# Explicit order edges on VectorE and ScalarE in a hybrid SSD and pooling decoder step: row product behind state updates, last gate half behind evictions, last weights' lower halves behind the last row block

## The chip, the cores and the metric

The kernel runs on one core of a Trainium2 chip. The core has a matrix engine (TensorE, PE in the profile), three elementwise engines (VectorE or DVE, ScalarE or ACT, GpSimd or POOL) and a queue that issues most transfers (SyncE, SP). The metric is the device time of one execution in microseconds (us). Instructions on one engine run in the order in which they stand in its program; engines wait for one another through semaphores.

## The reference, cut to what matters

One inference step of a two-layer trunk, in f32, for 1024 prompt tokens and 8 samples of 8 tokens each: 1088 columns in all (model width 1024, inner width 2048). Layer 0 is a Mamba-2 SSD layer, layer 1 a multi-scale causal pooling layer; each is RMSNorm with a conditioned scale and shift, a projection, a mixer, a gate and an output product, added to the residual. The parts that the change touches:

```python
def step(h, inp):                       # SSD: state from chunk to chunk (128 tokens)
    s, d = inp
    return d[..., None, None] * h + s, h
...
y_inter = jnp.einsum('bctgn,bctgr,bcgrpn->bctgrp', C, jnp.exp(acum), h_prev)
y = (y_intra + y_inter).reshape(b, L, H, P)
...
gated = (y * jax.nn.silu(z.astype(jnp.float32))).reshape(b, L, N_GROUPS, D_INNER // N_GROUPS)
gated = gated * lax.rsqrt(jnp.mean(gated * gated, axis=-1, keepdims=True) + EPS)
gated = gated.reshape(b, L, D_INNER) * norm_g.astype(jnp.float32)
return gated.astype(h.dtype) @ w_out, new_conv, new_ssm
...
return mixed.astype(h.dtype) @ w_out, up[:, -POOL_STATE:]      # pooling layer
...
y = rmsnorm(x, final_norm_g).astype(x.dtype)
```

`gated * rsqrt(mean) * norm_g` is the row product of the title. The new states, convolution tails and pooling tails are outputs too.

## The kernel before

Activations lie with channels on the 128 partitions and the 1088 tokens along the free axis. A product in f32 precision is made of three fast matmuls: each operand is split into an upper half (ScalarE copies it to a rounded type) and a lower half (VectorE subtracts the upper half from the raw tile), and TensorE adds upper times upper, upper times lower and lower times upper.

The program has four stages: a front part (normalisation, gates and part of the input projection), the scan of the SSD layer, the rest of that layer's output product with the pooling layer's projections and mixing, and the pooling layer's output product with the final normalisation.

**The scan.** `ssd_layer` goes over 8 groups of 4 heads (groups 0 to 7). `scan_group` is a generator: it handles chunks of 128 tokens in pairs and yields between them. In `front(c)` TensorE transposes the chunk's rows (`tr`, L573 and L576), ScalarE makes the decay mask `M` (L581, L582) and copies `Bt` (L593), VectorE makes `cb` (L584), multiplies `M` by it (L587) and makes `xd` (L589). `states(c, F)` lets TensorE write the chunk states `S` (L615) and updates the running state `h`: the first one of a group is a copy of `S` (L620), later ones are `hd = h * decay` on GpSimd (L623) and `h = hd + S` on VectorE (L624). `rows(c, F)` lets TensorE form the output rows `y` from `M` and `xd` (L636) and from the state (L640), and VectorE adds them into the group's tile (L607). After the last chunk the generator has three more parts, which belong to the end of the group: the gate, squares and mean with a transfer of the reciprocal root out to memory and back, broadcast to all partitions (`rs`, L742 and L745); then **the row product**, two VectorE instructions of 128x1088 (L749), each followed by a store of its result on the SP queue (`gyd`, L752).

`ssd_layer` steps these last parts inside the next group's scan (`rest` is the previous group's generator). Beside the scan stand the fill units of `beside()`: input projections of groups 1, 2, 3, 4 and 6 (matmuls L190 to L192), then three parts of the output product. The table `FILL` says how many fill units follow each scan step. The fill's projection tiles are evicted by ScalarE (L434, L436) and convolved by VectorE and ScalarE (L366 to L372).

**The output product of the SSD layer** sums over 16 row tiles in four parts. A row tile is loaded from `gyd` (`gr`, L766) and split: `gh` on ScalarE (L771), `gl` on VectorE (L772). Part 0 is loaded by the generator `self.prep`; `op_first` uses it first, with `gh` in L796 and L797 and `gl` in L801. The projection tile just ahead of it (group 6, tile 3) is written out by hand in `proj_group`: its three column blocks are evicted together, and one more step of `self.prep` follows, which issues the split of the last row tile of part 0 (the last gate half).

**The end of the kernel.** The pooling layer's output product goes over seven block products (`ORDER`). `block_steps` makes the row blocks `b`: ScalarE the upper half (L1187), VectorE the lower half (L1188). `ow_split` makes the weights' upper halves on ScalarE (L1231) and lower halves on VectorE (L1232). Before the last block product a loop in `pool_layer` fetches and splits the weights that are still missing. `contribute` adds a finished product into the residual (L1243).

**What sets the order.** Each engine's instructions are ordered by a scheduler, which takes the program's text as priority but lets an instruction stand earlier when it counts it as ready earlier. `tc.issue_after(ins)` adds an edge: what is issued inside it may not stand ahead of `ins` on the same engine. The edge adds no wait between engines.

Of the kernel before, what the change touches and what calls it, by code (L numbers as in the profile page):

```python
# [8 lines left out]
F32 = mybir.dt.float32  # L9
# [90 lines left out]
class Build:  # L100
# [296 lines left out]
    def proj_group(self, G):  # L397

        for ii in range(4):
            w = self.stream_next()  # L400
            raw = self.proj_begin(G, ii)
            if (G["g"], ii) == (BESIDE[-1], 3):
# [28 lines left out]
    def proj_evict(self, G, ii, raw, ps, c, end=True):  # L431
        nc, (a, n) = self.nc, CH[c]
        pn = min(a + n, NP) - a
        nc.scalar.activation(raw[:, 3 + a:3 + a + pn], ps[:, :pn], AF.Identity)  # L434
        if pn < n:
            nc.scalar.activation(raw[:, 1027:1115].rearrange("p (b w) -> p b w", w=11)[:, :, 3:11],  # L436
                                 ps[:, pn:n].rearrange("p (b i) -> p b i", i=8), AF.Identity)
            if end:
                self.proj_end(G, ii, raw, True)

    def gate_chunk(self, dst, c, ps):
# [83 lines left out]
    def scan_group(self, g, T):  # L525
# [84 lines left out]
        def states(c, F):  # L610
# [5 lines left out]
            for i in range(2):  # L616
                cd, Si = F[i][5], S[:, 256 * i:256 * i + 256]
                hn = gp.tile([P, 4, 64], F32, tag="h", bufs=3, name=self.name("h"))
                if h[-1] is None:
                    nc.vector.tensor_copy(hn.rearrange("p r q -> p (r q)"), Si)  # L620
                else:
                    hd = gp.tile([P, 4, 64], F32, tag="hd", bufs=1, name=self.name("hd"))
                    nc.gpsimd.tensor_tensor(out=hd, in0=h[-1], in1=cd.unsqueeze(2).to_broadcast([P, 4, 64]), op=ALU.mult)  # L623
                    nc.vector.tensor_tensor(out=hn, in0=hd, in1=Si.rearrange("p (r q) -> p r q", r=4), op=ALU.add)  # L624
                h.append(hn)

        def rows(c, F):
# [536 lines left out]
    def block_steps(self, m, rows):  # L1164
# [13 lines left out]
        for k in range(8):  # L1178
# [8 lines left out]
            nc.scalar.activation(t[:, :HALF], src, AF.Copy)  # L1187
            nc.vector.tensor_tensor(out=t[:, HALF:], in0=src, in1=t[:, :HALF].bitcast(F32), op=ALU.subtract)  # L1188
            out.append(t)
# [346 lines left out]
    def ssd_layer(self):  # L1536
# [118 lines left out]
    def pool_layer(self):  # L1655
# [239 lines left out]
```

## Time and profile before

| What | us |
|---|---|
| Median of 3 runs | 1607.51 (1605.86 to 1612.53) |
| The profiled execution's own time | 1606.84 |
| Its span, first to last instruction | 1605.1 |
| TensorE busy | 1579.7 |
| VectorE busy | 1292.1 |
| ScalarE busy | 789.5 |
| GpSimd busy | 515.3 |

How to read the rows: PE is TensorE, PEld its weight loads, DVE VectorE, ACT ScalarE, POOL GpSimd, SPq the queue of SyncE. A timeline row gives the start in us from the span's start, the duration of one instruction (of the whole run of them, where xN stands behind), the engine, the line, the operation with result and operands, and in brackets the idle time of the engine just ahead of it with what ended it. Durations include a tail that overlaps the next instruction, so an instruction takes up less of its engine than its duration. In a list of waits the three numbers are us in total, times, and the longest. The windows view gives for a stretch of time each engine's busy time and number of instructions, the clock granted to TensorE (1.00 is full), and the DMA engines' busy share and rate.

Numbers at the end of a tile's name tell buffers apart in the order listings; the profile leaves them out.

### The profile page before, as it was taken

The numbers are of one execution on the slowest core, as the hardware profiler recorded it, in microseconds if no ns is written. First come the engines' busy times: TensorE is split into PE (matmuls) and PEld (weight loads), VectorE is DVE, ScalarE is ACT, GpSimd is POOL, SyncE is SP. The second block draws the span as 40 slices with busy tenths as digits, with TensorE's granted clock in tenths as the row PEclk, the third lists the DMA queues.
The fourth block names the chain that finished last, engine by engine and source line by source line (L and its number), as shares of the span: only waits on it lengthen the run. The fifth ranks groups of instructions, "written<-read, shape, count | busy, mean of one in ns | idle before, by whom it ended". The sixth has DMA issues, their size and how long they took to land.

```text
span 1605.1 us, 30689 instructions
## 1 busy us (share of the span) xinstructions
PE 1579.7 (98%) x11946; PEld 1506.9 (94%) x11946; DVE 1292.1 (80%) x2152; ACT 789.5 (49%) x1512; POOL 515.3 (32%) x558
## 2 busy tenths in 40 slices
PE   9999999999999999999999999999999999999997
PEld 7899999998888888888899899999999999999997
DVE  6875879778788888888888867998889867677886
ACT  6663344456666766675545437632322233333364
POOL 0133456512231313130212232265666640000241
PEclk9999999999999999999999999999999999999999
DMA  9423232355555554678998542133323379565783
GB/s 352 166 100 110 69 111 91 102 186 158 187 161 171 156 177 150 214 252 292 303 338 296 206 135 86 53 134 114 115 102 104 111 233 373 152 172 178 161 173 121
DMA packets 122306, 275.58 MB, mean 172 GB/s; under 512 B 18193, under 2 KB 59313, under 8 KB 122161
## 3 DMA queue, kind: packets, MB, share of 16 engines
q1 hardware_dynamic: 118128, 260.90, 47.7%
q0 software_dynamic: 4032, 12.72, 4.7%
q8 instruction: 94, 1.54, 0.4%
q14 instruction: 52, 0.42, 0.1%
HBM read 201.12 MB, written 70.23 MB: 169 GB/s over the span
## 4 chain that ended last, share of the span: by engine, by line
PE 81%; DVE 7%; DMA 5%; issue 4%; ACT 2%; POOL 1%; SPq 0%; DVEq 0%; ACTq 0%; POOLq 0%
PE st L1042 10%; PE st L1040 10%; PE st L1041 10%; PE mm L190 10%; PE mm L191 9%; PE mm L192 9%; PE op L1259 2%; PE op L1260 2%; PE op L1258 2%; PE y L636 2%; PE y L640 2%; DMA rsd<-z 2%; PE S L615 2%; DMA rs<-rsd 1%; PE am L261 1%
## 5 line engine op out<-in xcount | busy, mean ns | idle before, releaser
L1040 PE MATMUL st<-hh,w 128*128 128x272 f32 x832 | 240.2, 289 | 1.0 <-ACT w L182 1.0
L1042 PE MATMUL st<-hh,w 128*128 128x272 f32 x832 | 240.4, 289 | 0.4 <-DVE w L184 0.4
L1041 PE MATMUL st<-hl,w 128*128 128x272 f32 x832 | 240.0, 288 | 0.0
L1040 PE MATMUL st<-t,w 128*128 128x272 f32 x624 | 179.6, 288 | 0.0
L1042 PE MATMUL st<-t,w 128*128 128x272 f32 x624 | 179.5, 288 | 0.0
L1041 PE MATMUL st<-t,w 128*128 128x272 f32 x624 | 179.2, 287 | 0.0
L190 PE MATMUL mm<-hh,wh 128*128 128x368 f32 (+1 forms) x528 | 178.6, 338 | 0.0
L191 PE MATMUL mm<-hl,wh 128*128 128x368 f32 (+1 forms) x528 | 173.1, 328 | 0.0
L192 PE MATMUL mm<-hh,wl 128*128 128x368 f32 (+1 forms) x528 | 172.9, 327 | 0.0
L1040 PEld LDWEIGHTS st<-hh,w 128*128 128x128 f32 x832 | 156.8, 188 | 1.4 <-ACT w L182 1.4
L1042 PEld LDWEIGHTS st<-hh,w 128*128 128x128 f32 x832 | 156.4, 188 | 0.9 <-DVE w L184 0.9
L1041 PEld LDWEIGHTS st<-hl,w 128*128 128x128 f32 x832 | 156.7, 188 | 0.0
L623 POOL TENSOR_TENSOR hd<-h,cd 128x256 f32<-128x256 f32 x56 | 46.9, 838 | 313.3 <-DVE h L624 154.6
L182 ACT ACTIVATE w<-wr 128x512 fp32r<-128x512 f32 x104 | 64.9, 629 | 166.4 <-PE st L1042 135.0
L1259 PE MATMUL op<-b,w 128*128 128x272 f32 x448 | 128.9, 288 | 0.7 <-DVE b L1188 0.7
L1258 PE MATMUL op<-b,w 128*128 128x272 f32 x448 | 129.4, 289 | 0.0
L1260 PE MATMUL op<-b,w 128*128 128x272 f32 x448 | 128.9, 288 | 0.0
L190 PE MATMUL mm<-gh,wh 128*128 128x368 f32 (+1 forms) x372 | 126.0, 339 | 0.2
L192 PE MATMUL mm<-gh,wl 128*128 128x368 f32 (+1 forms) x372 | 122.1, 328 | 0.0
L191 PE MATMUL mm<-gl,wh 128*128 128x368 f32 (+1 forms) x372 | 121.8, 327 | 0.1
L1040 PEld LDWEIGHTS st<-t,w 128*128 128x128 f32 x624 | 117.7, 189 | 0.1
L1042 PEld LDWEIGHTS st<-t,w 128*128 128x128 f32 x624 | 117.4, 188 | 0.0
(307 smaller groups left out, 4572.7 us busy)
## 6 DMA issues: line engine op xcount, KB each, us to landing
wr<-win SPq DMA_DIRECT2D x48, 512.0 KB, 3.8
acb<-acd SPq DMA_DIRECT2D x64, 256.0 KB, 4.2
wr<-pin SPq DMA_DIRECT2D x32, 512.0 KB, 3.7
wr<-pout SPq DMA_DIRECT2D x28, 512.0 KB, 4.9
x<-x1d SPq DMA_DIRECT2D x24, 544.0 KB, 5.8
x1d<-x SPq DMA_DIRECT2D x22, 544.0 KB, 4.5
wr<-pout POOLq DMA_DIRECT2D x20, 512.0 KB, 6.6
x<-xT SPq DMA_DIRECT2D x16, 544.0 KB, 6.8
```

The lines of the kernel that those rows point to most:

```text
L182: self.nc.scalar.activation(hi, src, AF.Copy)
L190: nc.tensor.matmul(ps[:, :n], hi[:, k, :], ah[:, a:a + n], start=first, stop=False)
L191: nc.tensor.matmul(ps[:, :n], hi[:, k, :], al[:, a:a + n], start=False, stop=False)
L192: nc.tensor.matmul(ps[:, :n], lo[:, k, :], ah[:, a:a + n], start=False, stop=last)
L615: nc.tensor.matmul(S[:, 256 * i:256 * i + 256], Bt, xde.rearrange("p r q -> p (r q)"), start=True, stop=True)
L623: nc.gpsimd.tensor_tensor(out=hd, in0=h[-1], in1=cd.unsqueeze(2).to_broadcast([P, 4, 64]), op=ALU.mult)
L1040: nc.tensor.matmul(ps[c][:, :QUART], hi[:, k], xh[:, t], start=(k == 0), stop=False)
L1041: nc.tensor.matmul(ps[c][:, :QUART], hi[:, k], xl[:, t], start=False, stop=False)
L1042: nc.tensor.matmul(ps[c][:, :QUART], lo[:, k], xh[:, t], start=False, stop=(k == 3))
L1258: nc.tensor.matmul(ps[:, :QUART], hi[:, k], xh, start=k == 0, stop=False)
L1259: nc.tensor.matmul(ps[:, :QUART], hi[:, k], xl, start=False, stop=False)
L1260: nc.tensor.matmul(ps[:, :QUART], lo[:, k], xh, start=False, stop=k == 7)
```

## The change

Three order edges are added, and the step at which the row product is issued is made the same for all groups.

- In `ssd_layer` the row product of the previous group is issued behind the fourth scan step of the next group (before: behind the fifth for groups up to 5). It gets edges behind the last state update that `states()` has issued so far (`self.hins`) and behind the fill unit's last instruction, where the unit hands one back. Its two `gyd` stores come with it.
- In `proj_group`, `proj_evict` returns its last eviction, and the step of `self.prep` that follows gets an edge behind it.
- In `pool_layer` the splits of the missing weights get an edge behind `self.lastb`, the last L1188 issued.

```diff
@@ proj_group
                 for c in range(3):
-                    self.proj_evict(G, ii, raw, ps[c], c, False)
-                next(self.prep)
+                    ins = self.proj_evict(G, ii, raw, ps[c], c, False)
+                with self.tc.issue_after(ins.ins):
+                    next(self.prep)
@@ proj_evict
-        nc.scalar.activation(raw[:, 3 + a:3 + a + pn], ps[:, :pn], AF.Identity)
+        ins = nc.scalar.activation(raw[:, 3 + a:3 + a + pn], ps[:, :pn], AF.Identity)
         if pn < n:
-            nc.scalar.activation(raw[:, 1027:1115]...
+            ins = nc.scalar.activation(raw[:, 1027:1115]...
...
+        return ins
@@ states
                 if h[-1] is None:
-                    nc.vector.tensor_copy(hn.rearrange("p r q -> p (r q)"), Si)
+                    ins = nc.vector.tensor_copy(hn.rearrange("p r q -> p (r q)"), Si)
                 else:
...
-                    nc.vector.tensor_tensor(out=hn, in0=hd, ...
+                    ins = nc.vector.tensor_tensor(out=hn, in0=hd, ...
                 h.append(hn)
+            self.hins = ins.ins
@@ block_steps
-            nc.vector.tensor_tensor(out=t[:, HALF:], in0=src, in1=t[:, :HALF].bitcast(F32), op=ALU.subtract)
+            self.lastb = nc.vector.tensor_tensor(out=t[:, HALF:], in0=src, in1=t[:, :HALF].bitcast(F32), op=ALU.subtract)
@@ ssd_layer
                 for j in range(n):
-                    next(self.fill)
-                    if i in (0, 3 + (g < 6)) and j == 0:
+                    ins = next(self.fill)
+                    if i == 0 and j == 0:
                         next(rest, None)
+                    elif i == 3 and j == 0:
+                        with self.tc.issue_after(self.hins), self.tc.issue_after(ins.ins) if ins else contextlib.nullcontext():
+                            next(rest, None)
@@ pool_layer
         while len(ws) < 28:
             self.ow_fetch()
-            self.ow_split()
+            with self.tc.issue_after(self.lastb.ins):
+                self.ow_split()
```

The new lines shift the numbers of later lines in the listings of the changed kernel by 2 to 6 (L620 of before is L622, L624 is L626, L749 is L752, L1188 is L1191).

The first place is VectorE early in group 1's scan. `xbc_3933` and `xbc_3945` are group 0's row tiles, `S_5116` the first chunk states of group 1 and `h_5119` the first running state. Before:

```order
L589 TENSOR_TENSOR xd_5083<-tr_5069,tkx_1451 128x512
L587 TENSOR_TENSOR M_5074<-M_5074,cb_5080 128x512
L749 SCALAR_TENSOR_TENSOR xbc_3933<-xbc_3933,vec,rs_5063 128x1088
L620 COPY h_5119<-S_5116 128x256
L584 TENSOR_TENSOR cb_5140<-tr_5129,kc 128x128
L589 TENSOR_TENSOR xd_5143<-tr_5129,tkx_1450 128x512
L624 TENSOR_TENSOR h_5121<-hd_5122,S_5116 128x256
L587 TENSOR_TENSOR M_5134<-M_5134,cb_5140 128x512
```

The same stretch after, and a second one further down, with the next pair's states (their numbers move by four):

```order
L591 TENSOR_TENSOR xd_5083<-tr_5069,tkx_1451 128x512
L589 TENSOR_TENSOR M_5074<-M_5074,cb_5080 128x512
L586 TENSOR_TENSOR cb_5140<-tr_5129,kc 128x128
L622 COPY h_5119<-S_5116 128x256
L589 TENSOR_TENSOR M_5134<-M_5134,cb_5140 128x512
L626 TENSOR_TENSOR h_5121<-hd_5122,S_5116 128x256
L591 TENSOR_TENSOR xd_5143<-tr_5129,tkx_1450 128x512
```

```order
L368 SCALAR_TENSOR_TENSOR raw_5196<-raw_5025,cwh,raw_5196 128x1112
L752 SCALAR_TENSOR_TENSOR xbc_3933<-xbc_3933,vec,rs_5063 128x1088
L368 SCALAR_TENSOR_TENSOR raw_5196<-raw_5025,cwh,raw_5196 128x1112
L752 SCALAR_TENSOR_TENSOR xbc_3945<-xbc_3945,vec,rs_5063 128x1088
L368 SCALAR_TENSOR_TENSOR raw_5196<-raw_5025,cwh,raw_5196 128x1112
L626 TENSOR_TENSOR h_5273<-hd_5274,S_5270 128x256
L586 TENSOR_TENSOR cb_5296<-tr_5285,kc 128x128
```

The first row product stood ahead of the first state copy; now it stands twelve rows lower, between the convolution's steps. The second one stood seven rows behind the next pair's second update (`h_5273` before); now it follows the first one and stands ahead of both updates of that pair (`h_5273`, which was `h_5269`, and `h_5277`). The groups 2, 3 and 4 show the same move.

The second place is ScalarE at the hand-written projection tile. `gh_8493` is the last gate half, `raw_8368` the tile that is evicted, `z_8230` the squares of group 4's second row tile. Before:

```order
L771 ACTIVATE gh_8458<-gr_8418 128x1088
L369 ACTIVATE raw_8124<-raw_8322 128x1112
L771 ACTIVATE gh_8493<-gr_8456 128x1088
L434 ACTIVATE raw_8368<-mm_8371 128x368
L434 ACTIVATE raw_8368<-mm_8372 128x368
L141 ACTIVATE wh_8503<-wr_8366 128x1024
L434 ACTIVATE raw_8368<-mm_8373 128x288
L436 ACTIVATE raw_8368<-mm_8373 128x8x8
L732 ACTIVATE z_8230<-xbc_7602 128x1088
L366 ACTIVATE raw_8754<-raw_8368,cwh 128x1112
```

After:

```order
L774 ACTIVATE gh_8458<-gr_8418 128x1088
L369 ACTIVATE raw_8124<-raw_8322 128x1112
L435 ACTIVATE raw_8368<-mm_8371 128x368
L435 ACTIVATE raw_8368<-mm_8372 128x368
L141 ACTIVATE wh_8503<-wr_8366 128x1024
L435 ACTIVATE raw_8368<-mm_8373 128x288
L437 ACTIVATE raw_8368<-mm_8373 128x8x8
L735 ACTIVATE z_8230<-xbc_7602 128x1088
L774 ACTIVATE gh_8493<-gr_8456 128x1088
L366 ACTIVATE raw_8754<-raw_8368,cwh 128x1112
```

The gate half moved behind the four evictions, and behind the squares `z_8230` as well.

The third place is VectorE ahead of the last block product. `b_18311` and `b_18329` are the last two row blocks, `w_18365` the lower half of the last weights. Before:

```order
L1188 TENSOR_TENSOR b_18311<-gin_16192,b_18311 128x544
L1232 TENSOR_TENSOR w_18365<-wr_18213,w_18364 128x1024
L1188 TENSOR_TENSOR b_18329<-gin_16194,b_18329 128x544
L1243 SCALAR_TENSOR_TENSOR x_17191<-op_18294,gat_279,x_17191 128x272
L1243 SCALAR_TENSOR_TENSOR x_16654<-op_18294,gat_279,x_16654 128x272
```

After:

```order
L1191 TENSOR_TENSOR b_18311<-gin_16192,b_18311 128x544
L1246 SCALAR_TENSOR_TENSOR x_17191<-op_18294,gat_279,x_17191 128x272
L1191 TENSOR_TENSOR b_18329<-gin_16194,b_18329 128x544
L1246 SCALAR_TENSOR_TENSOR x_16654<-op_18294,gat_279,x_16654 128x272
L1246 SCALAR_TENSOR_TENSOR x_17191<-op_18295,gat_279,x_17191 128x272
L1246 SCALAR_TENSOR_TENSOR x_16654<-op_18295,gat_279,x_16654 128x272
L1235 TENSOR_TENSOR w_18365<-wr_18213,w_18364 128x1024
```

The lower half moved from just ahead of the last row block to four rows behind it.

More of the change, by code (lines that the diff above doesn't have):

```diff
@@ L433, in proj_evict @@
         pn = min(a + n, NP) - a
-        nc.scalar.activation(raw[:, 3 + a:3 + a + pn], ps[:, :pn], AF.Identity)
+        ins = nc.scalar.activation(raw[:, 3 + a:3 + a + pn], ps[:, :pn], AF.Identity)
         if pn < n:
-            nc.scalar.activation(raw[:, 1027:1115].rearrange("p (b w) -> p b w", w=11)[:, :, 3:11],
+            ins = nc.scalar.activation(raw[:, 1027:1115].rearrange("p (b w) -> p b w", w=11)[:, :, 3:11],
                                  ps[:, pn:n].rearrange("p (b i) -> p b i", i=8), AF.Identity)
@@ L623, in states @@
                     nc.gpsimd.tensor_tensor(out=hd, in0=h[-1], in1=cd.unsqueeze(2).to_broadcast([P, 4, 64]), op=ALU.mult)
-                    nc.vector.tensor_tensor(out=hn, in0=hd, in1=Si.rearrange("p (r q) -> p r q", r=4), op=ALU.add)
+                    ins = nc.vector.tensor_tensor(out=hn, in0=hd, in1=Si.rearrange("p (r q) -> p r q", r=4), op=ALU.add)
                 h.append(hn)
+            self.hins = ins.ins
         def rows(c, F):
```

## Prediction

> **What bounds the kernel now.** I read the page's engine rows first, then the list of TensorE's waits, then the timelines around each wait that the change touches.
>
> ```profile
> span 1605.1 us, 30689 instructions
> PE 1579.7 (98%) x11946; PEld 1506.9 (94%) x11946; DVE 1292.1 (80%) x2152; ACT 789.5 (49%) x1512; POOL 515.3 (32%) x558
> ```
>
> TensorE is busy for 1579.7 of 1605.1 us. The change removes no matmul, so all that it can win lies in the other 25.4 us, plus matmuls that run at a lower clock than they could. No other engine is near its limit over the span; they count only where TensorE waits for them. The list of TensorE's waits says where:
>
> ```profile
> PE y L640 <- DVE h L620: 4.1, 4, 1.2
> PE S L615 <- ACT Bt L593: 2.2, 2, 1.4
> PE mm L796 <- ACT raw L434: 2.0, 1, 2.0
> PE op L1259 <- DVE b L1188: 0.7, 1, 0.7
> ```
>
> Four state copies hold TensorE for 4.1 us, two `Bt` copies for 2.2, the evictions at the hand-written tile for 2.0, the last row block for 0.7. Together 9.0 us of idle time, each at a place that the change touches. I cost them one by one.
>
> **Edit 1, groups 1 to 4.** The timeline of group 1, VectorE first, then TensorE:
>
> ```profile
> 435.15 0.68 DVE L587 TENSOR_TENSOR M<-M,cb 128x512 f32<-128x512 f32 x1
> 437.99 1.35 DVE L749 SCALAR_TENSOR_TENSOR xbc<-xbc,vec,rs 128x1088 f32<-128x1088 f32 x1 [2.16 <-DMA rs<-rsd]
> 439.25 0.42 DVE L620 COPY h<-S 128x256 f32<-128x256 f32 x1
> ...
> 441.70 0.86 DVE L607 SCALAR_TENSOR_TENSOR xbc<-xbc,vec,y 128x256 f32<-128x256 f32 x2
> ...
> 448.87 0.41 DVE L624 TENSOR_TENSOR h<-hd,S 128x256 f32<-128x256 f32 x1
> ```
>
> ```profile
> 435.82 0.70 PE L615 MATMUL S<-xd,Bt 128*128 128x256 f32 x2
> ...
> 438.15 0.38 PE L573 MATMUL tr<-xbc,xbc 128*128 128x128 f32 x2
> 439.73 0.66 PE L640 MATMUL y<-ea,h 128*64 128x128 f32 x8 [1.19 <-DVE h L620]
> ...
> 449.47 0.33 PE L191 MATMUL mm<-hl,wh 128*128 128x368 f32 x1
> 449.64 0.33 PE L192 MATMUL mm<-hh,wl 128*128 128x368 f32 x1
> 449.90 0.66 PE L640 MATMUL y<-ea,h 128*64 128x128 f32 x8
> ```
>
> The chunk states `S` are there at 435.82 + 0.70 = 436.52. VectorE is free from 435.83, but the row product stands next and waits 2.16 us for the broadcast `rs`; the copy of the state starts only at 439.25, and TensorE stands idle for 1.19 us at L640. After the change the copy follows a `cb` of some 0.3 us and starts when `S` is there, near 436.6. It is done near 437.1, and TensorE's own order moves L640 ahead to about 437.4: no wait. Between 438.15 and 439.73 lie 1.58 us where two transposes take about 0.22 of issue, so the gap costs 1.36, not 1.19; over four groups 4.1 + 4 x 0.17 = 4.8 us. Against that, L640 now stands between two projection matmuls instead of beside transposes. The change of form costs about 0.1 us there (0.26 from L192 at 449.64 to L640, against 0.17 from one projection matmul to the next); with something for the way back I take off 0.15 per group. Gross gain of this part: 4.8 - 0.6 = 4.2.
>
> What is late next? Both row products now stand ahead of the next pair's first state update. VectorE works without a gap from 441.70 to that update at 448.87, 7.2 us. After the change this stretch begins when the rows' sums are there, near 438.9, and holds two row products more. An instruction of 1.35 us occupies VectorE for about 1.26 (437.99 to 439.25), so the update starts at 438.9 + 7.2 + 2.5 = 448.6 and ends near 449.0. TensorE will ask for it, shifted by the gain and by its own order, near 449.7. The slack is about 0.7 us, and I cost it at nothing. If the cover is gone, the price is what a row product takes, at most 1.26 per group, 5.0 in all.
>
> The transfers move too. On SP's queue both `gyd` stores now stand ahead of the next weight load, and ScalarE takes those weights ahead of two evictions that it did first:
>
> ```profile
> 453.84 0.38 SPq L121 DMA_DIRECT2D wr<-win  x1
> 455.69 0.33 SPq L752 DMA_DIRECT2D gyd<-xbc  x1
> ```
>
> ```profile
> 458.67 0.22 ACT L436 ACTIVATE raw<-mm 128x64 f32<-128x64 f32 x1
> 460.14 1.06 ACT L141 ACTIVATE wh<-wr 128x1024 fp32r<-128x1024 f32 x1 [1.25 <-DMA wr<-win]
> ```
>
> The second product is done near 447.7, six us before the load was issued, so the store does not hold up the load. The evictions behind the weight split may wait 1.25 us longer, in four groups 0 to 5.0; they free a projection tile of which several are in rotation, so I take the lower side, 0.5 in all. Net of edit 1 in groups 1 to 4: -3.7.
>
> **Edit 1, groups 5 and 6.** The waits listed above include none there, and their row products have other work on both sides. The order shifts a `gr` load behind other transfers. I take 0, with 1.26 us per product as the bound on either side.
>
> **Edit 1, group 7.**
>
> ```profile
> 879.28 1.35 DVE L749 SCALAR_TENSOR_TENSOR xbc<-xbc,vec,rs 128x1088 f32<-128x1088 f32 x1 [1.46 <-DMA rs<-rsd]
> 879.62 1.05 ACT L141 ACTIVATE wh<-wr 128x1024 fp32r<-128x1024 f32 x1
> 884.19 0.70 PE L615 MATMUL S<-xd,Bt 128*128 128x256 f32 x2 [1.36 <-ACT Bt L593]
> 900.50 1.11 ACT L771 ACTIVATE gh<-gr 128x1088 fp32r<-128x1088 f32 x1 [1.85 <-DMA gr<-gyd]
> 901.83 0.70 PE L615 MATMUL S<-xd,Bt 128*128 128x256 f32 x2 [0.88 <-ACT Bt L593]
> ```
>
> The first wait of 1.36 comes from the row product ahead of `xd`, on which `Bt` follows. It moves behind, but a weights' lower half still stands ahead, and its upper half is done at 880.67; from there it is 1.1 us of lower half and about 1.8 us of small rows to `Bt`. TensorE would start near 883.6, 0.6 earlier. The next state update then has both row products ahead of it; 0.15 of new wait is my estimate. Gain 0.45, bounds 0 and 1.36. The second wait comes from a gate half that waits 1.85 us for its load ahead of `Bt`. In the new order `Bt` and a weight split stand ahead of this half: gain 0.88. Together -1.3.
>
> **Edit 2.** ScalarE, then TensorE, an earlier wait of TensorE, and the windows:
>
> ```profile
> 717.68 1.09 ACT L771 ACTIVATE gh<-gr 128x1088 fp32r<-128x1088 f32 x1
> 718.68 0.82 ACT L434 ACTIVATE raw<-mm 128x368 f32<-128x368 f32 x2
> ...
> 721.03 1.11 ACT L732 ACTIVATE z<-xbc 128x1088 f32<-128x1088 f32 x1 [0.16 <-DVE xbc L731]
> ```
>
> ```profile
> 719.19 0.52 PE L796 MATMUL mm<-gh,wh 128*128 128x368 f32 x1 [1.97 <-ACT raw L434]
> 719.51 0.51 PE L797 MATMUL mm<-gh,wl 128*128 128x368 f32 x1
> ...
> 723.74 0.33 PE L796 MATMUL mm<-gh,wh 128*128 128x368 f32 x1
> ```
>
> ```profile
> 359.00 0.66 PE L636 MATMUL y<-M,xd 128*64 128x128 f32 x8 [1.53 <-DVE M L587]
> ```
>
> ```profile
> 719.20:722.40 3.20, 3.20 (x12) 3.20 (x13) 3.20 (x4) 3.04 (x6) 1.45 (x2) 0.53 1.01 371
> 723.00:726.00 3.00, 3.00 (x23) 2.71 (x25) 3.00 (x5) 0.35 (x1) 0.00 (x0) 1.00 0.93 325
> 359.00:362.00 3.00, 2.99 (x24) 2.03 (x25) 2.57 (x6) 3.00 (x11) 0.00 (x0) 1.00 0.94 253
> ```
>
> TensorE waits 1.97 us for the evictions, which stand behind the last gate half; then it runs at a granted clock of 0.53 for some 3.2 us, which costs another 3.2 x 0.47 = 1.5. Without the half the evictions start at 717.68 and TensorE near 718.2, a wait of about 1.0. The clock stayed at 1.00 right behind the wait of 1.53 us at 359 (third window row), so I expect full pace. But the half now stands behind `z`, which cannot start before 721.03, and is done near 721.03 + 1.0 + 1.1 = 723.1. TensorE comes to it after eighteen matmuls of 0.17 and some transposes, near 721.9, and waits 1.2. Before, it came to the half at 723.74 with ten products of that kind still to do; now it starts on it 0.55 earlier with six to do, since the order lets the third row tile's products go first: 0.55 + 4 x 0.17 = 1.2 us. Gain 1.2; bounds: 0, if the new wait grows by as much, and 1.97 + 1.5 = 3.5, if the half is early.
>
> [...]
>
> **Edit 3.**
>
> ```profile
> 1569.61 1.22 DVE L1232 TENSOR_TENSOR w<-wr,w 128x1024 fp32r<-128x1024 f32 x1
> 1570.75 0.72 DVE L1188 TENSOR_TENSOR b<-gin,b 128x544 fp32r<-128x544 f32 x1
> 1569.73 0.66 ACT L1187 ACTIVATE b<-gin 128x544 fp32r<-128x544 f32 x1 [0.79 <-DVE b L1188]
> 1571.52 0.39 PE L1259 MATMUL op<-b,w 128*128 128x272 f32 x1 [0.68 <-DVE b L1188]
> ```
>
> The last row block needs its upper half, done at 1569.73 + 0.66 = 1570.39; it can start near 1570.45 instead of 1570.75. Gain 0.3 of the 0.68. The lower half of the weights comes about 2.5 us later; they belong to the fourth output tile of the product, three tiles on, which hides it. Bounds 0 and 0.68.
>
> **The sum.** -3.7 - 1.3 - 1.2 - 0.3 = -6.5 us against the profiled execution's 1606.84 gives 1600.3. The median of the runs shown stands 0.67 above that execution, so I forecast 1601.0, or 0.40% less. A measurement of this kernel can tell about 0.5%, 8.0 us, from no change.
>
> **Rivals.**
> - *More goes than I count.* All waits touched, 4.8 + 2.2 + 0.7, and the 3.5 of the gate half sum to 11.3 us: 1596. For it: VectorE gets back the 2.16 us that it stood still in each of four groups. Against it: the `z` ahead of the gate half and the weight split ahead of `Bt` are still there.
> - *The waits only move.* In groups 1 to 4 the pair's state update comes late behind both products: 5.0 us given back, 1606. For it: the slack is only about 0.7 us. Against it: VectorE's order there is walked row by row, and TensorE's L640 has itself moved down by eight matmuls.
> - *Slower.* The stores, now ahead of the weight load on SP's queue, hold it up, because the second product ends late. To turn -6.5 into +8.0 takes 14.5 us, 2.4 in each of groups 1 to 6: the product would have to end at 453.84 + 2.4 = 456.2, 8.5 us later than I walk it. That gives 1616. Nothing in the rows makes VectorE that late, and it decides only from there.
>
> **How the numbers follow.** My forecast (4 to 8 us gained) gets 0.57, more than that 0.27, the moved waits 0.10, slower 0.06. Forecast and moved waits are both within 0.5%: 0.67. The range goes from 1597, near the sum of all touched waits, to 1607, where the moved waits and the evictions give nearly everything back.
>
> **What would show it.** In the changed kernel's list of waits L640 on the state copy, L615 on `Bt` (but for 0.7) and L1259 at 0.68 should be gone; L796 should wait first about 1.0 us on an eviction and then about 1.2 on `gh`, at a clock of 1.00. A row of L640 waiting on L624 (four times, near 450 in group 1) would show the second rival; weight splits on ScalarE that wait several us for `win` in groups 1 to 6 the third; a granted clock near 0.5 behind the evictions would make me wrong on the pace in edit 2.

## The result, and the profile after

| | before | after |
|---|---|---|
| median, us | 1607.8 (1605.86 to 1612.53, 6 runs) | 1602.57 (1601.75 to 1603.61, 6 runs) |
| profiled execution, us (span) | 1606.84 (1605.1) | 1602.6 (1600.8) |
| TensorE busy, us | 1579.7 | 1579.9 |

The ratio is 0.997, with a 95% interval from 0.9956 to 0.9983: 5.2 us less by the medians, 4.2 by the two profiled executions. The forecast was 6.5 less and "within 0.5%".

TensorE's list of waits in the changed kernel (us in total, times, longest; lines of the changed kernel stand 2 to 6 further down):

```profile
PE S L617 <- ACT Bt L595: 1.4, 3, 0.7
...
PE mm L190 <- DVE x L816: 1.1, 1, 1.1
PE mm L799 <- ACT gh L774: 1.0, 1, 1.0
PE y L643 <- DVE h L626: 1.0, 1, 1.0
PE mm L799 <- ACT raw L435: 1.0, 1, 1.0
...
PE op L1262 <- DVE b L1191: 0.4, 1, 0.4
```

The line of the four state copies (4.1 us before) is gone, the evictions went from 2.0 to 1.0, the waits on `Bt` from 2.2 to 1.4, the last row block from 0.7 to 0.4. Three lines are new: the last gate half (L774), an eviction into `x` (L816), and a state update (L626). The first was forecast, the other two were not.

Early in group 1 VectorE and TensorE do what the order promised:

```profile
435.94 0.42 DVE L622 COPY h<-S 128x256 f32<-128x256 f32 x1 [0.34 <-PE S L617]
...
443.01 1.35 DVE L752 SCALAR_TENSOR_TENSOR xbc<-xbc,vec,rs 128x1088 f32<-128x1088 f32 x1
...
445.56 1.35 DVE L752 SCALAR_TENSOR_TENSOR xbc<-xbc,vec,rs 128x1088 f32<-128x1088 f32 x1
...
448.11 0.41 DVE L626 TENSOR_TENSOR h<-hd,S 128x256 f32<-128x256 f32 x1
```

```profile
436.64 0.43 PE L191 MATMUL mm<-hl,wh 128*128 128x352 f32 x1
436.99 0.66 PE L643 MATMUL y<-ea,h 128*64 128x128 f32 x8
```

The copy now waits for `S` and for nothing else; neither row product waits for `rs` any more, and the next pair's update starts at 448.11, where the prediction had 448.6.

Where the time went is read from five points that stand in both programs: the first group's mask (`y<-M,xd` at 359.00 before), the moment at which TensorE has nothing to do but wait for the evictions of the hand-written tile (start of the first `mm<-gh,wh` less its wait), the transposes behind that tile, the `Z` that ends group 6 (each group ends with one; this one has a wait of 0.29 ahead of it), and the first matmul into `pl`, the pooling layer's first projection. Before, then after:

```profile
728.17 0.38 PE L573 MATMUL tr<-xbc,xbc 128*128 128x128 f32 x2
...
846.11 0.64 PE L655 MATMUL Z<-h,ctm 128*32 128x256 f32 x8 [0.29 <-PE y L640]
...
981.28 0.33 PE L190 MATMUL pl<-hh,wh 128*128 128x368 f32 x1
```

```profile
358.02 0.66 PE L639 MATMUL y<-M,xd 128*64 128x128 f32 x8 [0.26 <-DVE M L589]
...
713.94 0.43 PE L799 MATMUL mm<-gh,wh 128*128 128x368 f32 x1 [1.00 <-ACT raw L435]
...
718.94 0.43 PE L799 MATMUL mm<-gh,wh 128*128 128x368 f32 x1 [1.04 <-ACT gh L774]
...
722.82 0.38 PE L575 MATMUL tr<-xbc,xbc 128*128 128x128 f32 x2
...
843.79 0.42 PE L658 MATMUL Z<-h,ctm 128*32 128x256 f32 x4 [0.29 <-PE y L643]
...
977.35 0.33 PE L190 MATMUL pl<-hh,wh 128*128 128x368 f32 x1
```

| Stretch | before | after | difference | forecast |
|---|---|---|---|---|
| start to the first group's mask | 359.00 | 358.02 | -1.0 | 0 |
| groups 1 to 4, to the wait for the evictions (717.22, 712.94) | 358.22 | 354.92 | -3.3 | -3.7 |
| hand-written tile | 10.95 | 9.88 | -1.1 | -1.2 |
| groups 5 and 6, to the `Z` of group 6 | 117.94 | 120.97 | +3.0 | 0 |
| group 7, to the pooling layer | 135.17 | 133.56 | -1.6 | -1.3 |
| the rest | 623.8 | 623.5 | -0.3 | -0.3 |

Everything that was forecast came, and a loss of 3.0 us that was not. The first row is no part of the change: the wait there is for an `acb` transfer (ScalarE waited 3.42 us for it before and 2.15 after), and over the fourteen profiles of this study, whatever their order, the mask's matmuls start between 357.96 and 359.59. Without that row the two profiles bear out 3.3 us of gain; the medians say 5.2, and what makes up the difference is not shown.

### The profile page after: what moved, and what is told of

Same layout as the page of the kernel before. It is cut to its first block, busy times and chain, and to the rows that moved or that the text cites. A ratio compares the mean times of both kernels' runs of the same rounds, so it can differ in the third digit from the quotient of the medians.

```text
span 1600.8 us, 30692 instructions
## 1 busy us (share of the span) xinstructions
PE 1579.9 (99%) x11946; PEld 1506.1 (94%) x11946; DVE 1291.7 (81%) x2152; ACT 789.6 (49%) x1512; POOL 518.8 (32%) x558
## 4 chain that ended last, share of the span: by engine, by line
PE 81%; DVE 8%; issue 4%; DMA 3%; ACT 3%; POOL 1%; SPq 0%; DVEq 0%; ACTq 0%; POOLq 0%
PE mm L190 10%; PE st L1045 10%; PE st L1043 10%; PE st L1044 10%; PE mm L191 10%; PE mm L192 10%; PE op L1262 2%; PE op L1263 2%; PE op L1261 2%; PE y L639 2%; DMA acb<-acd 2%; PE S L617 2%; PE y L643 2%; PE tr L578 1%; DVE xbc L359 1%
## 5 line engine op out<-in xcount | busy, mean ns | idle before, releaser
L1261 PE MATMUL op<-b,w 128*128 128x272 f32 x448 | 129.5, 289 | 0.0
```

What stands on the lines that cost most here:

```text
L1261: nc.tensor.matmul(ps[:, :QUART], hi[:, k], xh, start=k == 0, stop=False)
```

## The experiments

All are the changed kernel with the part shown put back or added; times are medians, the ratio is to the kernel before on the same chip. The stretches are measured between the same points in each run's profile, but in best1 eight `ms` matmuls and in evict_more four transposes of the tile stand on the other side of a point, which is worth about half a microsecond (the eight took 0.67 in edge_only, tail included; transposes start 0.11 us apart in the profile before):

| Run | median | ratio (95%) | groups 1-4 | tile | groups 5, 6 | group 7 |
|---|---|---|---|---|---|---|
| before | 1607.8 | 1 | 358.2 | 10.95 | 117.9 | 135.2 |
| changed kernel | 1602.57 | 0.9970 (0.9956 to 0.9983) | 354.9 | 9.88 | 121.0 | 133.6 |
| changed_again | 1603.24 | 0.9973 (0.9961 to 0.9985) | 355.3 | 9.82 | 121.3 | 132.9 |
| rows_only | 1604.75 | 0.9982 (0.9970 to 0.9993) | 356.0 | 8.84 | 122.2 | 133.1 |
| gate_only | 1607.92 | 0.9998 (0.9987 to 1.0008) | 359.4 | 9.35 | 121.5 | 134.0 |
| tail_only | 1607.25 | 0.9999 (0.9990 to 1.0008) | 358.6 | 9.88 | 119.7 | 136.0 |
| step_only | 1605.76 | 0.9987 (0.9976 to 0.9998) | 356.2 | 9.58 | 117.6 | 135.5 |
| edge_only | 1606.61 | 0.9996 (0.9988 to 1.0005) | 354.1 | 9.55 | 119.3 | 141.1 |
| rows_not56 | 1602.56 | 0.9975 (0.9966 to 0.9985) | 356.6 | 9.39 | 118.9 | 137.9 |
| rows_not6 | 1600.99 | 0.9963 (0.9951 to 0.9974) | 354.6 | 9.81 | 119.7 | 133.5 |
| rows_not6_again | 1602.43 | 0.9968 (0.9955 to 0.9981) | 354.6 | 9.70 | 119.7 | 133.2 |
| best1 | 1602.14 | 0.9966 (0.9954 to 0.9977) | 354.7 | 8.82 | 120.5 | 132.9 |
| evict_more | 1603.53 | 0.9980 (0.9971 to 0.9990) | 355.4 | 9.37 | 119.4 | 136.9 |
| late_evict | 1604.46 | 0.9981 (0.9972 to 0.9990) | 354.0 | 11.41 | 121.6 | 133.0 |

**One edit at a time.** rows_only has edit 1 without the other two (their lines as before):

```diff
-                with self.tc.issue_after(ins.ins):
-                    next(self.prep)
+                next(self.prep)
...
-            with self.tc.issue_after(self.lastb.ins):
-                self.ow_split()
+            self.ow_split()
```

> Edit 1 alone (row product behind the state updates in all groups); edits 2 and 3 undone. Theory P (each place keeps what it gained or lost): groups 1 to 4 gain 3.3 us, groups 5 and 6 lose 3.0, group 7 gains 1.5: 1.8 us under the kernel before, near 1606.0. TensorE still waits about 2.0 for the evictions at the hand-written tile and still runs about 3 us at half clock behind it. Rival D (VectorE has no time to spare in groups 5 and 6, so whatever arrives there early is given back, wherever it was gained): the stop at the evictions leaves VectorE time to catch up, so the waits on VectorE in groups 5 and 6 shrink to under 1 us together, and the gain is nearer 4: 1604.

It came out 2.5 us under the kernel before, between the two theories and nearer to P. Groups 1 to 4 gain 2.2 (3.1 but for the wait of 0.92 told below) and group 7 gains as in the changed kernel, and groups 5 and 6 lose more (122.2): two waits of 1.07 and 1.06 on evictions into `x`, 0.21 and 0.64 on `Bt` and the state, where the rival had under 1. The wait for the evictions was 1.07 here and not 2.0; TensorE had waited 0.92 at an earlier eviction, which makes 1.99 together. The clock stayed at 1.00, and the tile, in the order of the kernel before, took 8.84.

gate_only has edit 2 alone: the row product's step and order are those of the kernel before.

```diff
-                    elif i == 3 and j == 0:
-                        with self.tc.issue_after(self.hins), ...:
+                    elif i == 3 + (g < 6) and j == 0:
                             next(rest, None)
```

> Edit 2 alone (last gate half behind the evictions). Theory P: 1.1 us under the kernel before, near 1606.7; two waits of about 1.0 in place of one of 2.0, granted clock 1.00 behind them. Rival D: the 1.1 us are given back in groups 5 and 6 by a wait of TensorE on a VectorE result, no change: 1607.8. If the half clock has nothing to do with the length of the wait, the windows row behind the evictions shows 0.5 here too.

No change: the rival's number. The waits at the tile came as forecast (0.46 and 1.03, clock 1.00), and the gain was gone 12 us later, in group 5. There VectorE's row product waits for `rs` and the first state copy stands behind it. The rows are VectorE's, then TensorE's, then the windows (in order: us, busy time of PE, PEld, DVE, ACT, POOL, granted clock, DMA share, GB/s):

```profile
738.05 1.35 DVE L752 SCALAR_TENSOR_TENSOR xbc<-xbc,vec,rs 128x1088 f32<-128x1088 f32 x1 [3.00 <-DMA rs<-rsd]
...
739.88 0.41 DVE L622 COPY h<-S 128x256 f32<-128x256 f32 x1
```

```profile
740.35 0.75 PE L643 MATMUL y<-ea,h 128*64 128x128 f32 x8 [1.89 <-DVE h L622]
```

```profile
740.30:743.70 3.40, 3.35 (x17) 3.09 (x18) 2.47 (x5) 2.09 (x7) 2.21 (x2) 0.57 0.68 225
```

This is the fault that edit 1 mends in groups 1 to 4. In group 5 of the profile before it did not show as a wait, with the same order and TensorE at the same point at the same time: the chunk states `S` start at 736.19 there and at 736.16 here. What differs is the landing of `rs`. The same row product before:

```profile
735.53 1.35 DVE L749 SCALAR_TENSOR_TENSOR xbc<-xbc,vec,rs 128x1088 f32<-128x1088 f32 x1 [0.45 <-DMA rs<-rsd]
```

It started 2.5 us earlier, and the copy was done in time. The "waits listed above include none there" of the prediction was a fact about one execution.

tail_only has edit 3 alone (both other edits put back as above).

> Edit 3 alone. Theory P: TensorE's wait for the last row block shrinks from 0.7 to 0.4, the time by 0.3 us, which the runs can't tell from no change: 1606.5 to 1607.5. Rival: the lower half of the last weights, now 2.5 us later, is late for the fourth output tile, and a wait of TensorE on it shows; then no gain at all.

0.5 us under the kernel before, with an interval from 0.9990 to 1.0008: not to be told from no change, as expected. But its profile shows, with the order of the kernel before up to the tail, what a different execution does: 2.10 us of wait for the evictions with a granted clock of 1.00 behind it (719.20 to 722.40), and 1.65 in group 5 at the state copy, where the row product had waited 2.78 for `rs`.

```profile
PE y L642 <- DVE h L621: 5.6, 5, 1.7
...
PE mm L798 <- ACT raw L434: 2.1, 1, 2.1
```

That is a fifth state copy, group 5's, beside the four of the profile before. Groups 5 and 6 took 119.7 there against 117.9. At the tail TensorE waited three times some 0.4 us.

**The step or the edges.** step_only issues the row product at the fourth step and drops both edges; edge_only keeps the edges and the old step, which is the fifth in the scans of groups 1 to 5 only (in those of groups 6 and 7 it was the fourth before too).

```diff
 # step_only
                     elif i == 3 and j == 0:
-                        with self.tc.issue_after(self.hins), self.tc.issue_after(ins.ins) if ins else contextlib.nullcontext():
-                            next(rest, None)
+                        next(rest, None)
 # edge_only
-                    elif i == 3 and j == 0:
+                    elif i == 3 + (g < 6) and j == 0:
```

> The changed kernel without the two edges of edit 1: the row product is issued at the fourth step in all groups, but may stand anywhere (edits 2 and 3 stay). In this order the first product still stands ahead of the first state copy in groups 1 to 5 and 7. If the edges carry the gain: the waits at the state copies (4.1 us) are back, and the gate edit's gain is lost again in group 5, where the copy waits behind the product: 1607.5, as the kernel before. If issuing the step earlier carries it: near 1602.6.

> The changed kernel with the edges, but with the step of the kernel before (the fifth in groups 1 to 6). Both products then stand behind the next pair's state updates instead of ahead of them. If the edges carry the gain: as the changed kernel, 1602.6 within 1.5, with no wait at the state copies of groups 1 to 4. If the fourth step is needed too (products out of the way before VectorE fills up again): waits on VectorE or on late gate loads reappear in groups 1 to 6, 1604 or more.

Neither alone does it. Without the edges the waits at the state copies are back (0.76, 0.80, 0.19, 0.38) and groups 1 to 4 keep only about half of their gain. With the edges and the old step groups 1 to 4 are as good as in the changed kernel, or better (354.1), and so the edges carry that gain; but group 7 loses 7.5 us against the changed kernel. In its profile stand these waits of TensorE:

```profile
882.25 0.70 PE L617 MATMUL S<-xd,Bt 128*128 128x256 f32 x2 [2.00 <-ACT Bt L595]
...
920.87 0.67 PE L740 MATMUL ms<-z,ones 128*32 128x272 f32 x8 [0.74 <-DVE z L736]
```

with some 3.4 us near half clock behind the first; 0.36 and 0.47 at the group's begin add to them, and some 2 us of the loss stay unassigned. ScalarE stood ahead of that `Bt` for a late `acb` transfer (1.53 us). Group 7's own step is the same in both kernels; the later step of the groups ahead of it moves the `gyd` stores and what follows them on the queue. That this makes the transfer late is argued, not shown.

step_only shows one thing more. Its groups 5 and 6 take 117.6, as long as before (117.9), with no wait of TensorE over 0.3: the earlier step alone costs nothing there. The loss comes with the edges of these two groups, in the order that the scheduler then makes; evict_more has these edges too, in another order, and has neither of the two waits (119.4). Edges in groups 1 to 4 and 7 with the earlier step everywhere were not run.

**Groups 5 and 6.** rows_not56 and rows_not6 keep the row product of these groups, or of group 6 alone, where it was:

```diff
-                    elif i == 3 and j == 0:
-                        with self.tc.issue_after(self.hins), ...:
+                    elif i == (3 if g != 6 else 3 + (g < 6)) and j == 0:       # rows_not56: g not in (5, 6)
+                        with self.tc.issue_after(self.hins) if g != 6 else contextlib.nullcontext(), ...:
                             next(rest, None)
```

> The changed kernel, but in the scans of groups 5 and 6 the row product stays where it was in the kernel before (same step, no edges). Theory P (the moved row products and stores of these two groups cost 3.0 us there): 3.0 us under the changed kernel, near 1599.6; the waits on the eviction into x (1.1) and on the state update (1.0) are gone. Rival D (VectorE is full there in either order): same as the changed kernel, 1602.6 within 1, with waits of TensorE on VectorE of about 2 us in these groups, perhaps at other lines.

> The changed kernel, but only in group 6's scan the row product stays where it was before. Theory P: the wait on the state update in group 6 (1.0) comes from a gate half that waits 7.7 us for its load, since both stores and the load stand otherwise on the queue; with the old order it goes: 1.3 us under the changed kernel, near 1601.3, and the wait of 1.1 in group 5 stays. Rival D: same as the changed kernel, 1602.6 within 0.7.

> The changed kernel with group 6's row product as before, a second time, beside the changed kernel. Theory P: 1.3 us under the changed kernel of the same chip, interval clear of it; the gate half that waits 7.7 us for its load is not in the profile. Rival D: equal within 0.5 us.

> The changed kernel itself, on the same chip as the next run. Near 1602.6. Its profile tells which waits belong to its order and which to this or that execution: the waits on the gate half (1.0), on the eviction into x in group 5 (1.1) and on the state update in group 6 (1.0) should be there again; those at the first group's mask and at the copy in group 7 that follow a landing transfer may differ by 1 to 2 us.

In group 6 the cause is on ScalarE. In the changed kernel:

```profile
812.13 0.28 ACT L595 ACTIVATE Bt<-tr 128x128 f32<-128x128 f32 x1 [0.29 <-DVE xd L591]
820.07 1.11 ACT L774 ACTIVATE gh<-gr 128x1088 fp32r<-128x1088 f32 x1 [7.67 <-DMA gr<-gyd]
821.09 0.62 ACT L567 ACTIVATE ea<-acb 128x512 f32<-128x512 f32 x1
```

```profile
821.74 0.69 DVE L604 TENSOR_TENSOR ea<-xbc,ea 128x512 f32<-128x512 f32 x1 [1.82 <-ACT ea L567]
...
830.31 0.41 DVE L626 TENSOR_TENSOR h<-hd,S 128x256 f32<-128x256 f32 x1
```

```profile
830.78 0.44 PE L643 MATMUL y<-ea,h 128*64 128x128 f32 x4 [1.01 <-DVE h L626]
```

A gate half now stands early on ScalarE and waits 7.67 us for its `gr` load, with `ea`, the masks and `Bt` behind it; VectorE runs dry, and 9 us later TensorE waits for the state. In changed_again and late_evict, where the half waits 7.93 and 7.75, TensorE's wait stands at a `Bt` behind it (1.18 and 1.67). With group 6's product as before ScalarE goes on with them, and the half comes later with a wait of 1.35:

```profile
817.28 0.21 ACT L603 ACTIVATE cd<-acb 128x4 f32<-128x4 f32 x1 [4.71 <-POOL hd L625]
...
823.58 1.12 ACT L774 ACTIVATE gh<-gr 128x1088 fp32r<-128x1088 f32 x1 [1.35 <-DMA gr<-gyd]
```

The stretch shrinks from 121.0 and 121.3 to 119.7 in both profiles, by 1.3 to 1.6 as expected, and the wait is in neither. The medians are 1.6 (on another chip) and, beside the changed kernel on the same chip, 0.8 us lower, with intervals that overlap: shown in the profile, likely in the times.

In group 5 the sum fails. The old order there takes away the wait on the eviction into `x` (791.99 in the changed kernel, 1.06), and brings 0.89 at the state copy instead; the stretch is 0.8 shorter than in rows_not6 (118.9), but the median is the changed kernel's, the rival's number, and 1.6 us above rows_not6 (intervals overlap). Its profile shows where a gain can have gone: group 7 takes 137.9 there against 133.5, because of a `Bt` that had come to stand behind another row on ScalarE (last section).

The wait on the eviction into `x` is not a slower VectorE. Counted from the `Z` that ends group 5 (773.00 in the changed kernel, 776.72 before), VectorE starts that eviction 18.35 and 18.23 us later, the same within 0.12. TensorE asks for it 17.93 us after that `Z` in the changed kernel: its new order has put matmuls ahead of the `Z`. Between the tile's last point and this `Z` the trace has 376 matmuls in the kernel before and in every run without edges in group 5 (gate_only, tail_only, step_only, rows_not56), and none of these waits at `x`. It has 381 or 384 where group 5 has the edges (best1 another eight, the `ms` matmuls), and all of these wait 0.67 to 1.07 at `x`, but for evict_more, where VectorE starts the eviction 16.90 us after the `Z`.

Without their waits and the half clock, groups 5 and 6 still take about 1 us longer with the edges (118.9 in the changed kernel, 117.9 before). Half of that is in TensorE's order too: in these two groups it goes 76 times from a matmul into one tile to a matmul into another in place of 74 times, and these steps, from start to start and without the waits, take 14.5 us in place of 14.0. The rest I could not assign.

best1 corrects the order at the tile as well: group 4's second squares are issued behind the last gate half.

```diff
+        def squares(q):
+            nc.vector.tensor_tensor(out=xs[q], in0=xs[q], in1=zs[q], op=ALU.mult)
+            with self.tc.issue_after(self.ghins) if g == 4 and q else contextlib.nullcontext():
+                nc.scalar.activation(sq[q], xs[q], AF.Square)
+            if q:
+                nc.vector.tensor_tensor(out=sq[0], in0=sq[0], in1=sq[1], op=ALU.add)
...
                 with self.tc.issue_after(ins.ins):
                     next(self.prep)
+                self.defer()                        # squares(1) of group 4
```

> The changed kernel with two corrections: group 6's row product as in the kernel before, and at the hand-written tile the second half of group 4's squares behind the last gate half instead of ahead of it. Theory P: the wait for the gate half (1.0) goes, and group 6's wait (1.0) with it: 1.0 under the run without group 6 and 2.3 under the changed kernel, near 1600.0. Rival D (VectorE gives it back in group 5): the wait on the eviction into x in group 5 grows from 1.1 to about 2, and the time stays at that of the run without group 6, 1601.0.

The wait for the gate half is gone, and 0.92 at `gl`, the lower half of a gate row, has come in its place:

```profile
722.05 0.93 PE L812 MATMUL mm<-gl,wh 128*128 128x368 f32 x4 [0.92 <-DVE gl L783]
```

The tile and groups 5 and 6 together take 129.3 against 129.5 in rows_not6. Nothing gained: neither theory's place was right, the next wait was a lower half on VectorE. No run beat both kernels by an interval clear of the changed kernel's; rows_not6 has the lowest ratios, 0.9963 and 0.9968.

**The half clock.** evict_more does the first eviction four times over, late_evict cuts the split just ahead of the evictions into 16 pieces:

```diff
 # evict_more
-                    ins = self.proj_evict(G, ii, raw, ps[c], c, False)
+                    for _ in range(1 if c else 4):
+                        ins = self.proj_evict(G, ii, raw, ps[c], c, False)
 # late_evict (pieces is set for the third gate row of part 0)
-        self.nc.scalar.activation(hi, raw, AF.Copy)
+        step = 68 if self.pieces else TOK
+        for a in range(0, TOK, step):
+            self.nc.scalar.activation(hi[:, a:a + step], raw[:, a:a + step], AF.Copy)
```

> The changed kernel with the first of the three evictions at the hand-written tile done four times over (the result is the same). TensorE's wait for the evictions grows from 1.0 to some 2.8 us. Theory C (a wait of more than about 1.6 us is followed by 3.4 us at half clock): windows show 0.5 behind it, and the sequence is 2.2 us longer than in the changed kernel, near 1604.8. Rival N (the half clock of the kernel before came from something else): the clock stays 1.00, the wait for the gate half is gone instead, and the sequence is only 0.5 us longer: 1603.1.

> The changed kernel with the split of the third gate row tile cut into 16 pieces on ScalarE (same result), just ahead of the evictions at the hand-written tile. The evictions come 1 to 2 us later, TensorE's wait for them grows from 1.0 to 2.0 to 3.0 us. Theory C (a wait of about 1.7 us or more is followed by some 3.4 us at half clock): 0.5 in the windows behind it, and the tile's end comes 2.5 us later than in the changed kernel: near 1605.0. Rival N (no such effect): clock 1.00 there, the end comes at most 1.2 us later, since the wait for the last gate half shrinks: 1603.6.

evict_more missed its aim: the copies were spread over the order, and the wait split into 1.25 and 0.84, without a half clock there. late_evict hit it:

```profile
715.16 0.48 PE L803 MATMUL mm<-gh,wh 128*128 128x368 f32 x1 [2.43 <-ACT raw L437]
```

```profile
715.00:717.00 2.00, 1.84 (x7) 1.84 (x8) 2.00 (x3) 2.00 (x6) 0.23 (x1) 0.60 0.78 308
717.00:720.00 3.00, 3.00 (x16) 2.98 (x15) 3.00 (x3) 3.00 (x3) 1.98 (x2) 0.69 1.01 318
720.00:723.00 3.00, 3.00 (x24) 2.32 (x23) 2.82 (x5) 0.53 (x2) 0.00 (x0) 1.00 0.97 360
```

The clock fell behind the longer wait (0.60 and 0.69 in the windows) as theory C has it, and the tile took 11.41 against 9.82 and 9.88: 1.5 to 1.6 us more, less than the 2.5 expected, since the wait for the last gate half went. In the medians it is 1.2 beside the changed kernel on the same chip (intervals overlap). The rival's clock of 1.00 is refuted.

The lengths of all waits over 1.6 us in the scans of the fourteen profiles, with what the windows show behind them: 1.76, 1.79, 1.89, 1.97, 2.00, 2.43 and 2.61 were each followed by about 3.4 us near half clock (a window of 10 us at 0.83); 1.65 (twice), 1.67, 1.99, 2.09 and 2.10 were not. Up to 1.53 none was. At the tail of tail_only three waits of about 0.4 within 2.2 us were followed by it:

```profile
1571.00:1574.00 3.00, 1.91 (x11) 1.25 (x9) 2.07 (x5) 1.45 (x3) 0.00 (x0) 1.00 0.01 3
1574.00:1577.40 3.40, 3.34 (x15) 3.34 (x16) 3.40 (x8) 0.56 (x2) 0.00 (x0) 0.54 0.00 0
```

The first row holds nearly all of the three waits, the second the half clock.

So the length of a wait alone does not part these cases: behind 2.10 us the clock stayed at 1.00, behind 1.76 it did not. In the profile before, a stretch at half clock lasts 3.413 us, from 719.40 to 722.82, and the next one starts at 1600.04, 257 times as long after its end; in rows_not56 the stretches start at 360.73, 893.20 and 1599.76, which is 156 and then 207 steps of 3.413 us apart. Here are the steps of this length around the tile's wait in the profile before, and then in tail_only, counted back by 251 from 1574.24, where its stretch at half clock starts:

```profile
715.99:719.40 3.41, 1.44 (x9) 1.16 (x8) 3.41 (x6) 3.41 (x6) 0.00 (x0) 1.00 0.92 351
719.40:722.81 3.41, 3.41 (x13) 3.41 (x13) 3.41 (x4) 3.25 (x6) 1.45 (x2) 0.50 0.98 351
...
714.09:717.50 3.41, 2.98 (x19) 2.69 (x17) 2.72 (x4) 2.99 (x3) 0.00 (x0) 1.00 0.93 341
717.50:720.91 3.41, 1.74 (x11) 1.65 (x11) 3.41 (x5) 3.35 (x7) 0.12 (x1) 1.00 0.96 393
720.91:724.32 3.41, 3.41 (x22) 3.22 (x21) 3.41 (x4) 2.33 (x2) 1.35 (x2) 1.00 1.00 292
```

Before, the wait of 1.97 lies in one step and leaves TensorE 1.44 us busy of 3.41; the next step runs at 0.50. In tail_only the longer wait of 2.10 is cut in two by the edge at 717.50, no step has more than 1.68 us idle, and the clock stays at 1.00. Counted so, all cases of the scans part: behind each of the seven steps with 1.76 us or more of idle time TensorE ran the next step at half clock, and behind no step with up to 1.68 us did it. That the idle time within a step matters, and not the length of the wait, is an estimate from these numbers. Two stretches at half clock outside the scans do not fit at first sight, the one at the tail of tail_only and one at 22.09 in rows_not6; the step ahead of each has 1.15 us idle. At the tail that is counted too low, by an estimate: 13 matmuls fall into the step, two of them begun ahead of it, and in a row they start 0.125 us apart, so that at most 1.6 us of work leave 1.8 or more idle; the rest of the busy time is the tail of single matmuls (0.29 us long each). The other one stays open.

## Why the prediction was right, and where it was off

The time lay in the range and 1.6 us above the forecast; "within 0.5%" was right. That it came so near is in part luck: the steps of the sum, as the profiles measure them, give 3.3 us and not 6.5, and 1.0 at the start and another 1.0 between profiles and medians, which no step has, bring it to 5.2. By its own steps:

- *Edit 1, groups 1 to 4, -3.7.* Right: -3.3 in the profile of the result, and 2.2 to 4.2 less than before in the other runs that have it, but for rows_not56 (1.6 less, with a stretch at half clock from 360.73). The copy started at 435.94 and no L643 waited there. The second rival (the waits only move to the pair's update) fell: the update stood at 448.11 and TensorE had no wait on it. What was new, 0.95 in two waits on `Bt`, was not in the sum. Against step_only, where the copies wait again, it is the edges that carry this gain.
- *Group 7, -1.3.* Right: -1.6. The wait of 0.88 is gone, that of 1.36 is 0.41.
- *Edit 2, -1.2.* The size was right, the reason only in part. The tile took 1.1 less, with the two waits forecast (1.0 and 1.0). But tail_only, whose order there is that of the kernel before, shows the tile at 9.88 with a wait of 2.10 and full clock: as long as with the edit, and rows_only shows 8.84 with a wait of 1.07. The moved half takes from one wait what it adds to the other, and the gain is the half clock, which stood behind the wait of 1.97 in the profile before (0.50) and not behind that of 2.10 in tail_only (1.00). The prediction counted from 723.74, a time with the half clock in it, as if that belonged to the order; that the tile came out at 1.1 is luck. Alone the edit gained nothing in the median.
- *Edit 3, -0.3.* Its wait shrank by 0.3 in the result's profile, as in six more of the eleven profiles that have the edit. The other four show two or three waits of that size in a row (changed_again 0.38 and 0.37), as much as before or more; the medians can't tell.
- *Edit 1, groups 5 and 6, 0.* This step failed. Measured: +3.0. Group 6's part, 1.3 to 1.6, is the gate half that the new order puts early on ScalarE, where it waits for its load 7.67 us; the prediction saw that "The order shifts a `gr` load behind other transfers" and did not ask what stands behind the half on ScalarE. Group 5's part is the wait of 1.06 on the eviction into `x`, which TensorE's own new order asks for sooner, and about 1 us of which half is in that order and the rest unassigned. The bound given, 1.26 per product on either side, holds the loss (four products, 5.0).

The sum had no term for the start; 1.0 us of the profiled gain is a transfer that landed earlier, and has nothing to do with the change.

## What to carry to other kernels

A list of waits shows where the engine that bounds the kernel waited in that execution; a place with the same order and no wait in the list is not safe where it hangs on a transfer (group 5 here: no wait before, 1.89 us in gate_only with TensorE there at the same time, because `rs` let VectorE start 2.5 us later). When an instruction is moved, follow what the scheduler moves with it on the engines that it does not run on: the loss here was a gate half on ScalarE, put ahead of others, waiting for a load, and five matmuls on TensorE. Edits that each clear one wait are worth their sum only if the next place takes the early arrival; run them alone and together.

## What the runs showed that was not expected

- One short wait can cost twice: behind waits of 1.76 to 2.61 us TensorE ran 3.4 us at half clock, some 1.7 us lost on top, in seven of thirteen cases above 1.6 us; these seven are the ones with 1.76 us or more of idle time within one step of 3.413 us, where the others have at most 1.68. This may explain part of why executions of one order differ by 4 us: rows_not56 ran between 1601.31 and 1607.77, and its profile, of the slowest, has waits of 1.79 and 2.61 with some 3.4 us near half clock behind each.
- One place in ScalarE's order decided whether group 7 gained. `es` waits for a 128 KB `acb` load late in that group. In the changed kernel, then in evict_more:

```profile
888.88 0.28 ACT L595 ACTIVATE Bt<-tr 128x128 f32<-128x128 f32 x1 [0.98 <-DVE xd L591]
891.23 0.26 ACT L571 ACTIVATE es<-acb 128x32 f32<-128x32 f32 x1 [2.07 <-DMA acb<-acd]
...
890.37 0.26 ACT L572 ACTIVATE es<-acb 128x32 f32<-128x32 f32 x1 [3.80 <-DMA acb<-acd]
890.53 0.26 ACT L596 ACTIVATE Bt<-tr 128x128 f32<-128x128 f32 x1
```

With `Bt` ahead the wait did not lengthen group 7, also where `es` waits 3.25 (rows_not6, 133.5). With `Bt` behind, as in evict_more and rows_not56, TensorE waits 1.76 and 2.61 for it, with some 3.4 us near half clock after, and group 7 takes 136.9 and 137.9 in place of 133.6. Neither run's edit touches group 7: the scheduler had moved it.
